# Down projections of a hybrid decoder trunk: the weights' differences and low parts moved from GpSimd to VectorE

## The chip, the cores and the metric

The kernel runs on one core of a Trainium2 chip. The metric is device time in microseconds (us). A core has five engines with an in-order queue each: TensorE (PE in the profile; PEld is its weight load), VectorE (DVE), ScalarE (ACT), GpSimd (POOL) and SyncE (SP), which here issues nearly all DMAs. The engines run side by side and wait for one another through semaphores.

## The reference

Two layers over 16 meta tokens and 1024 tokens of width 1024, all in float32: a Mamba-2 mixer and a convolutional gated FFN, then stick-breaking attention and a second FFN. What the change touches is the last product of each FFN, the down projection:

```
D_MODEL, D_FF, FFN_CONV = 1024, 2816, 3

def _conv_ffn(u, w_up, conv_w, conv_b, w_down):
    h = _causal_dwconv(u @ w_up, conv_w, conv_b)
    g, val = jnp.split(h, 2, axis=-1)
    return (jax.nn.silu(g) * val) @ w_down

for layer in range(DEPTH):          # DEPTH = 2
    ...                             # layer 0: SSD mixer; layer 1: attention
    h = h + _conv_ffn(_rmsnorm(h, ffn_norm[layer]), ffn_w_up[layer], ...,
                      ffn_w_down[layer])
```

## The kernel before, in words

**Three products for one.** TensorE multiplies a rounded float32 format (F32R). To keep float32 precision, each operand is split into a rounded high part and the rest: ScalarE copies `x` into `hi` with the rounding, and another engine makes `lo = x - hi`. `mm3` (from L153) then issues three matmuls: high by high (L156), weights' high by the tokens' low part (L157), weights' low by the tokens' high part (L158).

**Stages.** The kernel runs the mixer, the up projection of layer 0 (`up`), its down projection (`down`), the attention, and `up` and `down` of layer 1. Token tiles have F = 260 columns in layer 0 and 256 in layer 1.

**The down projection.** `down` (from L946) takes the first 16 of the 22 blocks of 128 of the inner width and multiplies them with a Strassen-Winograd scheme: the tokens' half-matrices are `b11, b12, b21, b22` (two token halves by two halves of the inner width), the weights' are `a11` to `a22`, and seven products (i = 1, 7, 6, 5, 3, 4, 2, in this order) take the place of eight. There are two rounds, and in each round two sets (`Set`, x = 0 and 1) whose products are summed in PSUM: 28 operand sets per down, 14 pairs. The rows that remain (`rows`, six blocks) are multiplied in the ordinary way at the end (`weights`, `tokens`), while `sums` adds the seven sums into the stream.

`operands(i)` makes what one product of one set needs. In place, on tiles of 128 x 1024, it forms the difference of weights (L989, L992, L995, L998; on GpSimd as `pt`) and of tokens (L990, L993, L996, L1000; on VectorE as `tt`). Then come four instructions: ScalarE rounds the weights (L1004, `wh`), GpSimd makes their low part (L1005, `wl`), ScalarE rounds the tokens (L1006, `gh`), VectorE makes their low part (L1007, `gl`). `wh` and `wl` have three buffers each. In `weights` (L1062, L1063) the ordinary blocks are split in the same way, the low part on GpSimd.

`part` issues the matmuls of one accumulator: per operand set 48 matmuls of 260 columns in layer 0 (eight accumulators, all eight PSUM banks), 24 of 512 columns in layer 1 (four). After the second set of a pair, `add` (L1052, L1054) empties the bank: VectorE adds it to a sum in SBUF, or, where a sum begins (products 1, 5, 6 and 7 in the first round), ScalarE copies it. The sums of `sums` are L1024, the rounding and low parts of `tokens` are L1073 and L1074. GpSimd also makes the differences and low parts of the up projection's weights (`up_weights`, L859 and nearby), and VectorE its convolutions and sums (L282, L901, L909).

**Order.** Outside the attention, the order on each engine is set by a planner that lays the instructions out by its own costs when the kernel is built. One edge is set by hand: `behind_up` ties an instruction behind `last_up`, the last product of the up projection's gate on VectorE (L901), without a semaphore, so that in the same engine's queue it comes after it. Before the change it holds the tokens' first difference of product 7 (L990).

Of the kernel before, what the change touches and what calls it, by code (L numbers as in the profile page):

```python
# [8 lines left out]
F32 = mybir.dt.float32  # L9
# [60 lines left out]
class Trunk:  # L70
# [875 lines left out]
    def down(self, layer, gd, hd, pool, after):  # L946
# [3 lines left out]
        nc, a, F = self.nc, self.a, FNS[layer]  # L950
        H, S = D // 2, 2 * F
        parts = [(0, S)] if S <= 512 else [(0, F), (F, F)]
        tt = nc.vector.tensor_tensor
        pt = nc.gpsimd.tensor_tensor
        ADD, SUB = ALU.add, ALU.subtract
        half = lambda j: slice(S - S * j, 2 * S - S * j)

        def behind_up(ins):

            nosync = mybir.DependencyInfo(mybir.DependencyClass.NoSync, mybir.DependencyReason.DATA)  # L960
            self.tc.add_manual_dep(ins.ins, self.last_up.ins.name, nosync, reason="behind the up projection")

        def pair(t, w):
            return t[:, : 2 * w].rearrange("p (q c) -> p q c", q=2)

        class Set:
# [16 lines left out]
            def operands(me, i):  # L983

                b, w = me.b, me.w
                b11, b12, b21, b22 = b[0, 0], b[0, 1], b[1, 0], b[1, 1]
                a11, a12, a21, a22 = w[0, 0], w[0, 1], w[1, 0], w[1, 1]
                if i == 7:
                    pt(a21, a11, a21, op=SUB)  # L989
                    behind_up(tt(b12, b22, b12, op=SUB))  # L990
                elif i == 6:
                    pt(a21, a22, a21, op=SUB)  # L992
                    tt(b11, b11, b12, op=ADD)  # L993
                elif i == 5:
                    pt(a11, a11, a21, op=ADD)  # L995
                    tt(b12, b22, b11, op=SUB)  # L996
                elif i == 3:
                    pt(a21, a12, a21, op=SUB)  # L998
                elif i == 4:
                    tt(b11, b21, b11, op=SUB)  # L1000
                x, y = {1: (b11, a11), 7: (b12, a21), 6: (b11, a21), 5: (b12, a11), 3: (b22, a21), 4: (b11, a22), 2: (b21, a12)}[i]
                gh, gl = (pair(self.Q(z, F32R), QW // 2)[:, :, :S] for z in ("gh", "gl"))
                wh, wl = (self.wp.tile([P, 1024], F32R, tag=z, name=self.nm(z)) for z in ("wh", "wl"))
                nc.scalar.activation(wh, y, AF.Copy)  # L1004
                pt(wl, y, wh.bitcast(F32), op=SUB)  # L1005
                nc.scalar.activation(gh, x, AF.Copy)  # L1006
                tt(gl, x, gh.bitcast(F32), op=SUB)  # L1007
                return gh, gl, wh, wl
# [50 lines left out]
        def weights(b, hi, lo):  # L1059
            w32 = self.wp.tile([P, 1024], F32, tag="w32", name=self.nm("w32"))  # L1060
            nc.sync.dma_start(w32, a["w_down"][layer, b])
            nc.scalar.activation(hi, w32, AF.Copy)  # L1062
            pt(lo, w32, hi.bitcast(F32), op=SUB)  # L1063
            ws.append((hi, lo))

        def tokens(x):
# [23 lines left out]
        for m in range(0, len(plan), 2):  # L1090
            r, i, _ = plan[m]
            last = r + 1 == len(rounds)
            ps = {}
            if r == 0 and i == 7:
                for f in range(KD):
                    nc.sync.dma_start(h[f][:, : 2 * S] if f < 4 else h[f][:, half(0)], hd[f] if f < 4 else hd[f, :, half(0)])
            if last and i == 2:
                h22 = [self.Q("h22") for _ in range(2)]
                h22 = [h22[f // 2][:, f % 2 * S : f % 2 * S + S] for f in range(4)]
                for f in range(4):  # L1100
                    nc.sync.dma_start(h22[f], hd[4 + f, :, half(1)])
            for x in range(2):
                make(m + x + 1)
                if last and i == 4 and x:
                    weights(rows[0], *own())
                if last and i == 2 and not x:
                    tokens(0)
                    weights(rows[1], *own())
                    weights(rows[2], *(self.Q(z, F32R)[:, :D] for z in ("wh", "wl")))
                    for b in rows[3:]:  # L1110
                        weights(b, *common())
                for t, f in ((t, f) for t in range(len(parts)) for f in range(4)):
                    if x == 0:
                        ps[t, f] = next(kinds)("acc")
                    part(ps[t, f], made[m + x], f, t, x == 0)
                    if x == 1:
                        add(i, f, t, ps.pop((t, f)), r == 0)
                del made[m + x]
# [445 lines left out]
```

## Time and profile before

| | |
|---|---|
| median of 3 runs | 3022.47 us (3021.38 to 3026.99) |
| the profiled execution | 3024.83 us, of which the span of the trace is 3023.1 us |
| granted TensorE clock, mean | 0.981 |
| first down projection in the trace | first matmul at 1356.7 us |
| second down projection in the trace | first matmul at 2752.82 us |

How to read the profile: times count from the start of the span. A row of the timeline gives start and duration in us, engine, line, operation, output and inputs with their shapes, and the number of instructions merged; in brackets the idle time of the engine before it and what ended that. A row of the windows gives from and to, length, busy time of an engine with its count of instructions, the clock that TensorE was granted (1.00 is full), the share of time that the DMA engines were busy, and GB/s. A row of waits names who waited for whom: total us, times, longest. A row of groups gives line, engine, operation, count, then total busy us and mean ns of one, then idle time before. TensorE's matmuls are pipelined: one lasts longer than the distance between two starts.

### The profile page before, as it was taken

The numbers are of one execution on the slowest core, as the hardware profiler recorded it, in microseconds if no ns is written. First come the engines' busy times: TensorE is split into PE (matmuls) and PEld (weight loads), VectorE is DVE, ScalarE is ACT, GpSimd is POOL, SyncE is SP. The second block draws the span as 40 slices with busy tenths as digits, with TensorE's granted clock in tenths as the row PEclk, the third lists the DMA queues.
The fourth block names the chain that finished last, engine by engine and source line by source line (L and its number), as shares of the span: only waits on it lengthen the run. The fifth ranks groups of instructions, "written<-read, shape, count | busy, mean of one in ns | idle before, by whom it ended". The sixth has DMA issues, their size and how long they took to land.

```text
span 3023.1 us, 57199 instructions
## 1 busy us (share of the span) xinstructions
PE 2875.1 (95%) x21855; PEld 2733.1 (90%) x21855; DVE 2158.8 (71%) x3994; ACT 1621.9 (54%) x3308; POOL 1403.3 (46%) x1282
## 2 busy tenths in 40 slices
PE   7999999989989999998999999999997999998988
PEld 4998998889979999998998999999797999997778
DVE  5686868875376665568966888888748665568895
ACT  4555555553245555554334888877735555554432
POOL 1254444532415666658733222222234676667751
PEclk9999999999999999999999999999998999999999
DMA  5243323313222222243132222221331222225231
GB/s 161 75 118 86 109 78 111 113 53 139 74 78 64 78 80 77 84 160 132 47 117 72 60 65 65 68 59 52 129 112 64 85 76 79 77 84 176 91 105 56
DMA packets 125891, 272.76 MB, mean 90 GB/s; under 512 B 15888, under 2 KB 55440, under 8 KB 125616
## 3 DMA queue, kind: packets, MB, share of 16 engines
q1 hardware_dynamic: 120304, 258.17, 27.1%
q10 hardware_dynamic: 4048, 6.36, 0.6%
q0 software_dynamic: 1264, 4.57, 0.4%
q8 instruction: 172, 2.82, 0.4%
q14 instruction: 103, 0.84, 0.1%
HBM read 200.93 MB, written 53.21 MB: 84 GB/s over the span
## 4 chain that ended last, share of the span: by engine, by line
PE 52%; DVE 13%; ACT 4%; issue 3%; DMA 2%; POOL 0%; SPq 0%; DVEq 0%; ACTq 0%; POOLq 0%
PE p L156 9%; PE p L157 9%; PE p L158 9%; PE acc L157 4%; PE acc L156 4%; PE acc L158 4%; DVE gl L1007 3%; PE po L1314 2%; PE pj L156 2%; PE pj L158 2%; PE pj L157 2%; PE lg L1272 1%; DVE kp L1285 1%; PE wT L1299 1%; ACT kp L1275 1%
## 5 line engine op out<-in xcount | busy, mean ns | idle before, releaser
L156 PE MATMUL pj<-uh,wh 128*128 128x348 f32 (+2 forms) x1536 | 507.3, 331 | 16.1 <-DVE qs L1223 7.1
L157 PE MATMUL pj<-ul,wh 128*128 128x348 f32 (+2 forms) x1536 | 498.7, 325 | 0.0
L158 PE MATMUL pj<-uh,wl 128*128 128x348 f32 (+2 forms) x1536 | 496.2, 323 | 0.0
L157 PE MATMUL p<-bl,fh 128*128 128x262 f32 (+1 forms) x1408 | 401.0, 285 | 14.0 <-DVE bl L827 14.0
L156 PE MATMUL p<-bh,fh 128*128 128x262 f32 (+1 forms) x1408 | 401.3, 286 | 4.2 <-ACT fh L858 3.5
L158 PE MATMUL p<-bh,fl 128*128 128x262 f32 (+1 forms) x1408 | 399.3, 284 | 0.0
L859 POOL TENSOR_TENSOR fl<-x,fh 128x1024 fp32r<-128x1024 f32 x88 | 212.7, 2418 | 306.4 <-ACT fh L858 277.5
L150 POOL TENSOR_TENSOR wl<-w,wh 128x1024 fp32r<-128x1024 f32 (+2 forms) x80 | 164.6, 2060 | 327.1 <-ACT wh L149 327.0
L156 PEld LDWEIGHTS pj<-uh,wh 128*128 128x128 f32 x1536 | 292.0, 190 | 23.8 <-DVE qs L1223 9.2
L157 PE MATMUL p<-bl,wh 128*128 128x262 f32 (+1 forms) x1056 | 301.8, 286 | 8.5 <-DVE bl L827 8.5
L156 PE MATMUL p<-bh,wh 128*128 128x262 f32 (+1 forms) x1056 | 301.9, 286 | 6.3 <-ACT bh L826 6.3
L158 PE MATMUL p<-bh,wl 128*128 128x262 f32 (+1 forms) x1056 | 301.2, 285 | 0.0
L157 PEld LDWEIGHTS pj<-ul,wh 128*128 128x128 f32 x1536 | 292.6, 190 | 1.4 <-issue 0.5
L158 PEld LDWEIGHTS pj<-uh,wl 128*128 128x128 f32 x1536 | 291.9, 190 | 0.3 <-issue 0.2
L157 PEld LDWEIGHTS p<-bl,fh 128*128 128x128 f32 x1408 | 268.0, 190 | 16.1 <-DVE bl L827 15.9
L282 DVE SCALAR_TENSOR_TENSOR c<-p,params,c 128x260 f32<-128x260 f32 (+1 forms) x440 | 207.9, 481 | 94.4 <-ACT c L278 92.6
L156 PEld LDWEIGHTS p<-bh,fh 128*128 128x128 f32 x1408 | 268.4, 191 | 6.0 <-ACT fh L858 3.9
L158 PEld LDWEIGHTS p<-bh,fl 128*128 128x128 f32 x1408 | 267.4, 190 | 0.1
L157 PE MATMUL acc<-gl,wh 128*128 128x260 f32 (+1 forms) x672 | 217.9, 326 | 19.8 <-DVE gl L1007 19.8
L909 DVE TENSOR_TENSOR p<-p,ft 128x262 f32<-128x262 f32 (+1 forms) x176 | 76.8, 436 | 221.6 <-ACT ft L906 128.9
L384 DVE TENSOR_TENSOR h<-h,acc 128x256 f32<-128x256 f32 (+4 forms) x232 | 102.6, 450 | 175.1 <-PE acc L158 172.5
L156 PE MATMUL acc<-gh,wh 128*128 128x260 f32 (+1 forms) x672 | 215.0, 325 | 8.7 <-DVE p L1054 5.4
(309 smaller groups left out, 8539.4 us busy)
## 6 DMA issues: line engine op xcount, KB each, us to landing
w<-in_w_up SPq DMA_DIRECT2D x88, 512.0 KB
w<-in_w_down SPq DMA_DIRECT2D x44, 512.0 KB
w<-in_w_in SPq DMA_DIRECT2D x40, 512.0 KB
E<-ea_d SPq DMA_DIRECT2D x32, 464.0 KB
D<-acs_d SPq DMA_DIRECT2D x32, 420.5 KB
g<-c SPq DMA_DIRECT2D x88, 130.0 KB
g<-c SPq DMA_DIRECT2D x88, 128.0 KB
b<-g SPq DMA_DIRECT2D x16, 520.0 KB
```

The lines of the kernel that those rows point to most:

```text
L150: nc.gpsimd.tensor_tensor(wl[:, :n], w32[:, :n], wh[:, :n].bitcast(F32), op=ALU.subtract)
L156: mm(out, wh, uh, start=first, stop=False, skip_group_check=joins)
L157: mm(out, wh, ul, start=False, stop=False, skip_group_check=joins)
L158: mm(out, wl, uh, start=False, stop=last, skip_group_check=joins)
L282: nc.vector.scalar_tensor_tensor(to, ps[:, o + i : o + i + n], wcol(i), out, op0=ALU.mult, op1=ALU.add)
L384: self.nc.vector.tensor_tensor(h[f][:, o], h[f][:, o], ps[:, :n], op=ALU.add)
L859: tt(lo[:, :n], t, hi[:, :n].bitcast(F32), op=ALU.subtract)
L909: add = lambda o, x, y: tt(o[:, :N], x[:, :N], y[:, :N], op=ALU.add)
L1007: tt(gl, x, gh.bitcast(F32), op=SUB)
L1272: nc.tensor.matmul(ps[:nt, :m], part[:, c0 : c0 + nt], ks[a][:, s0 : s0 + m], start=x == 0, stop=x == 1)
L1275: nc.scalar.activation(kp[:nt, :m], ps[:nt, :m], AF.Sigmoid, scale=self.rt[2][:nt, i : i + 1])
L1314: nc.tensor.matmul(po[64 * a : 64 * a + 64, w], v[: CH[c][1], c, 64 * a : 64 * a + 64], wt[a][: CH[c][1], c, :nt], start=x == 0, stop=x == ...
```

## The change

In `down`, the name `pt` (GpSimd) goes, and everything that it did is done by VectorE (`tt`): the four kinds of weight differences, the low parts `wl` of every operand set, and the low parts of the ordinary blocks. GpSimd has no instruction left in `down`. The first weight difference of product 7 is tied behind the up projection's last VectorE instruction, as the tokens' difference next to it was already.

```
-        pt = nc.gpsimd.tensor_tensor
...
                 if i == 7:
-                    pt(a21, a11, a21, op=SUB)
+                    behind_up(tt(a21, a11, a21, op=SUB))
                     behind_up(tt(b12, b22, b12, op=SUB))
                 elif i == 6:
-                    pt(a21, a22, a21, op=SUB)
+                    tt(a21, a22, a21, op=SUB)
                     tt(b11, b11, b12, op=ADD)
                 elif i == 5:
-                    pt(a11, a11, a21, op=ADD)
+                    tt(a11, a11, a21, op=ADD)
                     tt(b12, b22, b11, op=SUB)
                 elif i == 3:
-                    pt(a21, a12, a21, op=SUB)
+                    tt(a21, a12, a21, op=SUB)
...
                 nc.scalar.activation(wh, y, AF.Copy)
-                pt(wl, y, wh.bitcast(F32), op=SUB)
+                tt(wl, y, wh.bitcast(F32), op=SUB)
                 nc.scalar.activation(gh, x, AF.Copy)
                 tt(gl, x, gh.bitcast(F32), op=SUB)
...
             nc.scalar.activation(hi, w32, AF.Copy)
-            pt(lo, w32, hi.bitcast(F32), op=SUB)
+            tt(lo, w32, hi.bitcast(F32), op=SUB)
             ws.append((hi, lo))
```

More of the change, by code (lines that the diff above doesn't have):

```diff
@@ L953, in down @@
         tt = nc.vector.tensor_tensor
-        pt = nc.gpsimd.tensor_tensor
         ADD, SUB = ALU.add, ALU.subtract
@@ L988, in operands @@
                 if i == 7:
-                    pt(a21, a11, a21, op=SUB)
+                    behind_up(tt(a21, a11, a21, op=SUB))
                     behind_up(tt(b12, b22, b12, op=SUB))
                 elif i == 6:
-                    pt(a21, a22, a21, op=SUB)
+                    tt(a21, a22, a21, op=SUB)
                     tt(b11, b11, b12, op=ADD)
                 elif i == 5:
-                    pt(a11, a11, a21, op=ADD)
+                    tt(a11, a11, a21, op=ADD)
                     tt(b12, b22, b11, op=SUB)
                 elif i == 3:
-                    pt(a21, a12, a21, op=SUB)
+                    tt(a21, a12, a21, op=SUB)
                 elif i == 4:
@@ L1004, in operands @@
                 nc.scalar.activation(wh, y, AF.Copy)
-                pt(wl, y, wh.bitcast(F32), op=SUB)
+                tt(wl, y, wh.bitcast(F32), op=SUB)
                 nc.scalar.activation(gh, x, AF.Copy)
@@ L1062, in weights @@
             nc.scalar.activation(hi, w32, AF.Copy)
-            pt(lo, w32, hi.bitcast(F32), op=SUB)
+            tt(lo, w32, hi.bitcast(F32), op=SUB)
             ws.append((hi, lo))
```

## The prediction

> **What bounds the kernel now.** I read the page first: span, busy shares.
>
> ```profile
> span 3023.1 us, 57199 instructions
> PE 2875.1 (95%) x21855; PEld 2733.1 (90%) x21855; DVE 2158.8 (71%) x3994; ACT 1621.9 (54%) x3308; POOL 1403.3 (46%) x1282
> ```
>
> The profiled execution took 3024.83 us; the sum below starts there. The median shown, 3022.47, lies 2.4 us lower, inside the spread of the three runs. TensorE is the bound nearly everywhere, so a change is worth what it takes from TensorE's waits. So next come the stretches of the two down projections, TensorE alone: length, busy time (matmuls), granted clock, then DMA.
>
> ```profile
> 1365.00:1405.00 40.00, 30.03 (x228) 0.91 0.17 68
> 1425.00:1430.00 5.00, 4.43 (x35) 1.00 0.44 159
> 1430.00:1460.00 30.00, 30.00 (x254) 1.00 0.29 89
> 1460.00:1505.00 45.00, 39.61 (x312) 0.96 0.04 13
> 1530.00:1550.00 20.00, 16.79 (x125) 0.91 0.52 168
> 2765.00:2800.00 35.00, 25.19 (x98) 0.90 0.17 57
> 2805.00:2870.00 65.00, 65.00 (x282) 1.00 0.31 104
> 2870.00:2875.00 5.00, 3.14 (x14) 1.00 0.00 2
> 2900.00:2910.00 10.00, 9.32 (x37) 1.00 0.32 108
> 2925.00:2945.00 20.00, 14.59 (x90) 0.83 0.37 130
> ```
>
> 1430 to 1460 and 2805 to 2870 are undisturbed: 254/30 = 8.47 matmuls per us (260 columns) and 282/65 = 4.34 (512 columns). At those rates the matmuls of the other stretches would need less time than they took. The losses, idle and lower clock together:
> First down: 40 - 228/8.47 = 13.1 (start), 0.9 and 45 - 312/8.47 = 8.2 (middle), 20 - 125/8.47 = 5.2 (tail): 27.4 us.
> Second down: 35 - 98/4.34 = 12.4 (start), 1.8 and 1.5 (middle). The tail mixes widths, so I take idle 5.4 plus 14.59 x 0.17 = 2.5 for the clock: 7.9. Together 23.6 us.
> So 51.0 us is all that better operands could return. Who is waited for, the first three rows in the first down, the others in the second (total, times, longest):
>
> ```profile
> PE acc L157 <- DVE gl L1007: 10.0, 4, 5.6
> PE acc L156 <- DVE p L1054: 5.4, 4, 2.7
> PE acc L156 <- DVE h L1054: 3.7, 4, 1.8
> ...
> PE acc L157 <- DVE gl L1007: 9.8, 4, 4.9
> PE acc L158 <- POOL wl L1005: 2.4, 2, 1.9
> ```
>
> VectorE (gl, and the adds of L1054 that empty the banks) is late, GpSimd seldom. That looks like a reason not to give VectorE more. The timeline of the two engines says otherwise (start, duration).
>
> ```profile
> 1346.22 1.24 DVE L1007 TENSOR_TENSOR gl<-b,gh 128x1040 fp32r<-128x1040 f32 x1 [3.35 <-ACT gh L1006]
> 1347.38 0.43 DVE L909 TENSOR_TENSOR p<-p,ft 128x262 f32<-128x262 f32 x1
> 1361.20 6.16 DVE L990 TENSOR_TENSOR b<-b,b 128x1040 f32<-128x1040 f32 x2
> 1370.61 3.39 DVE L1007 TENSOR_TENSOR gl<-b,gh 128x1040 fp32r<-128x1040 f32 x1
> 1373.92 3.40 DVE L993 TENSOR_TENSOR b<-b,b 128x1040 f32<-128x1040 f32 x1
> 2757.16 6.14 DVE L990 TENSOR_TENSOR b<-b,b 128x1024 f32<-128x1024 f32 x2
> ...
> 1337.56 2.40 POOL L1005 TENSOR_TENSOR wl<-w,wh 128x1024 fp32r<-128x1024 f32 x1 [0.30 <-ACT wh L1004]
> 1369.55 3.35 POOL L1005 TENSOR_TENSOR wl<-w,wh 128x1024 fp32r<-128x1024 f32 x1
> 1372.86 3.37 POOL L995 TENSOR_TENSOR w<-w,w 128x1024 f32<-128x1024 f32 x1
> ```
>
> The same gl takes 1.24 us with GpSimd idle (the next instruction starts 1.16 later) and 3.39 while GpSimd runs beside it. GpSimd's own goes from 2.40 to 3.35. One instruction on each engine thus takes 3.31 us start to start; two on VectorE alone would take 2.32. Moving work *to* the late engine should make it earlier.
>
> **The change, part by part.**
>
> *Moved: low parts.*
>
> ```profile
> L1005 POOL TENSOR_TENSOR wl<-w,wh 128x1024 fp32r<-128x1024 f32 x56 | 162.1, 2902 | 99.6 <-ACT wh L1004 99.6
> ```
>
> 56 here, and by the code 12 of L1063 and 32 differences (L989, L992, L995, L998; 16 per down): 100 instructions. VectorE gains 100 x 1.16 = 116 us and loses the stretching, about 2.2 us on each gl or b that overlapped. All of it must hide under the matmuls, so it is judged by rate. TensorE's rate from its timeline:
>
> ```profile
> 1356.70 0.28 PE L156 MATMUL acc<-gh,wh 128*128 128x260 f32 x1
> 1357.41 0.28 PE L156 MATMUL acc<-gh,wh 128*128 128x260 f32 x1
> 1374.05 0.59 PE L157 MATMUL acc<-gl,wh 128*128 128x260 f32 x1 [5.62 <-DVE gl L1007]
> ...
> 2762.80 0.39 PE L157 MATMUL acc<-gl,wh 128*128 128x512 f32 x1
> 2763.73 0.39 PE L158 MATMUL acc<-gh,wl 128*128 128x512 f32 x1
> 2769.99 0.79 PE L157 MATMUL acc<-gl,wh 128*128 128x512 f32 x1 [4.95 <-DVE gl L1007]
> ```
>
> Six starts in 0.71 us are 0.118 each; an operand set has 48 matmuls, 5.7 us. In the second down four starts in 0.93 make 0.2325; 24 matmuls, 5.6 us.
>
> *Start.* Up's last VectorE work ends at 1361.2; the tie puts the difference of a21 behind it, where GpSimd did it during the up stage. Product 1 of both sets keeps TensorE busy from 1356.70 for 2 x 5.7 = 11.4 us, to 1368.1. Now gl starts at 1370.61 and TensorE goes on at 1374.05. After: a21 and b12 of both sets, 4 x 1.16 from 1361.2, end at 1365.8, and wl and gl of the first set at 1368.2. ScalarE's two roundings lie under the second set's differences. So even in the poorer order the stall is near 0.1 us; with one or two differences of product 6 ahead of gl (as L993 could be) 1 to 2.5. The second down has the same order: free at 2757.2, six instructions later 2764.2, and TensorE's work lasts to 2769.99 - 4.95 = 2765.0. I keep 1.5 us of each start. After that products 7, 6 and 5 need 4 x 1.16 = 4.6 us of VectorE per set (ScalarE empties the banks in this round) against 5.7: VectorE gets ahead. Returned: 11.6 + 10.9 = 22.5.
>
> *Middle (second round).* VectorE also empties banks:
>
> ```profile
> 1459.87 2.75 DVE L1007 TENSOR_TENSOR gl<-b,gh 128x1040 fp32r<-128x1040 f32 x1
> 1462.55 0.75 DVE L1054 TENSOR_TENSOR p<-p,acc 128x260 f32<-128x260 f32 x2
> 1473.29 2.77 DVE L1007 TENSOR_TENSOR gl<-b,gh 128x1040 fp32r<-128x1040 f32 x1
> ```
>
> From one pair's gl to the next pair's is 13.4 us now. After: 8 x 1.16 + 8 adds of at most 0.375 = 12.3, against 11.4 of TensorE: still short by 0.9 in each of three pairs, 2.7 us, part of it covered because operands are made up to two sets ahead (wh and wl have three buffers). In products 3, 4, 2 and 1, with one difference per set or none, VectorE needs at most 10. The second down's four adds of twice the width I put at the same 3.0, against 2 x 5.6. I keep 2.0 and 1.5 of the 9.1 and 3.3: returned 8.9.
>
> *Tail.* The last low parts (L1063) ran beside the sums of L1024:
>
> ```profile
> 1530.67 2.22 DVE L1024 TENSOR_TENSOR h<-h,p 128x520 f32<-128x520 f32 x1
> 1535.92 1.30 DVE L1024 TENSOR_TENSOR h<-h,p 128x520 f32<-128x520 f32 x2
> ...
> 1529.40 5.71 POOL L1063 TENSOR_TENSOR wl<-w,wh 128x1024 fp32r<-128x1024 f32 x2 [0.83 <-ACT wh L1062]
> ```
>
> Two of L1063 stretched the L1024 beside them from 0.65 to 2.22; on VectorE they cost 2 x 1.16 themselves. Bounds: nothing returned, or all 13.1 of both tails. Nearest row: two stretched sums (3.1) against 2.3 of new work, a small gain, but the waits on POOL wl go too. I take half: 6.5.
>
> *Up's end.* The wl of product 1 is not tied. Two per down now lie between up's convolutions on VectorE, which idles 3.35 us ahead of the gl at 1346.22, so cost 0 to 2 x 1.16 per down. I take 1.2 each: -2.4. No DMA is moved, and SP's queue is passed by nothing. w and b tiles come free earlier, so the second round's loads may start earlier; the start has the room for them (DMA share 0.17 in both).
>
> Sum: 22.5 + 8.9 + 6.5 - 2.4 = 35.5 us, 3024.8 - 35.5 = 2989 us. Of 51.0, 13.1 stays.
>
> *The clock.* After the 5.62 us wait a matmul lasts 0.59, and the stretch shows 0.91; but 1460 to 1505 shows 0.96 although its longest wait is 2.7, and lost 8.2 with 5.4 idle. So I let short waits cost clock too: about a third of the 13.1 that stays. The Trainium skill, "TensorE: Matmul & The Clock Gate" (Part 1, the HAM clock gate), has the clock halve only after an idle window of about 3.4 us; the first row agrees, the second speaks for more than that. By the rule the waits I leave, all shorter, would cost no clock, and the time would be some 4 us lower, 2985, an estimate from that page.
>
> **Rivals.**
> (a) *VectorE becomes the bound.* For: 12.3 against 11.4, one in-order queue for operands, adds and sums. Then middle and tails stay as they are, a start keeps 3 us: returned 25.5 - 6 - 2.4 = 17, 3008 us. Against: the queue is slower today.
> (b) *No change.* The first low parts go early into VectorE's queue and hold up's convolutions:
>
> ```profile
> 1356.99 1.06 ACT L1004 ACTIVATE wh<-w 128x1024 fp32r<-128x1024 f32 x1 [0.73 <-DMA w<-in_w_down]
> ```
>
> wl of set 2 needs this wh (end 1358.05). Put ahead of the convolutions of 1349, it would hold them 9 to 10 us per down, and the starts return little: 35.5 - 2 x 10 - 13 = 3, 3022 us. Against: ScalarE's order stands 0.73 us off the landing, so the planner knows the load's time.
> (c) *Slower: adds behind waiting operands.* wl waits for wh, wh for TensorE to free a buffer; GpSimd bore 99.6 us of that. If VectorE's queue has wl and gl ahead of the adds that free the next product's banks, TensorE waits 2 x 1.16 + 1.06 = 3.4 us per pair. There are 28 pairs; it decides from 35.5/28 = 1.3 us per pair on. If every second pair pays, 47.6 - 35.5 = 12: 3037 us. Against: gl has the same wait already, right behind.
>
> **How the numbers follow.** Mine 0.65, (a) 0.17, (b) 0.08, (c) 0.10. 0.2% (6 us) is about what a measurement tells from no change. Faster 0.82, same 0.08, slower 0.10. The low end is all 51 returned less a little, 2976; the high end reaches past (a), to 3014, which leaves (b) and (c) out. Mine alone: 2976 to 3001.
>
> **What would show it.** gl, b, w and wl on VectorE near 1.2 us in both downs; no GpSimd there. The matmul after product 1 follows with under 2.5 us of wait, and the 40 us from there hold about 320 matmuls, not 228, at full clock. Middle: waits on L1054 of 1 to 3 us. I am wrong if VectorE's instructions stay above 2 us (the stretching had another cause), if L1054 is waited for in every pair, or if up's end slides later than 1361 and 2757.

## The result, and the profile after

| | before | after |
|---|---|---|
| median | 3022.18 us (4 runs, 3021.38 to 3026.99) | 2971.34 us (4 runs, 2970.31 to 2975.13) |
| ratio, with its 95% interval | | 0.9829 (0.9817 to 0.9840) |
| the profiled execution | 3024.83 us, span 3023.1 us | 2970.31 us, span 2968.4 us |
| granted TensorE clock, mean | 0.981 | 0.988 |

The change returns 50.8 us by the medians, 1.7%. The kernel is faster, as forecast, but by 17.7 us more than forecast, and its time lies 4.7 us below the low end of the range. In the changed kernel the lines of `down` stand one lower (`wl` is L1004, `gl` L1006, `add` L1051 and L1053, the differences L988 to L999, the tail's low part L1062).

First the page of the kernel after: span, and busy time of each engine.

```profile
span 2968.4 us, 57155 instructions
PE 2853.7 (96%) x21855; PEld 2718.1 (92%) x21855; DVE 2121.7 (71%) x4094; ACT 1622.3 (55%) x3308; POOL 1110.3 (37%) x1182
```

VectorE has 100 instructions more and is busy 37 us less. The 100 take 100 x 1.22 = 122 us there, so everything else on VectorE became 159 us shorter: 1.6 us for each instruction that left GpSimd.

Next the windows of the kernel after, TensorE alone, over the stretches that the prediction summed (from and to, length, busy with its count of matmuls, clock, DMA share, GB/s).

```profile
1365.00:1405.00 40.00, 38.92 (x323) 1.00 0.45 155
1430.00:1460.00 30.00, 30.00 (x253) 1.00 0.00 1
1460.00:1505.00 45.00, 45.00 (x378) 1.00 0.33 107
1505.00:1550.00 45.00, 45.00 (x377) 1.00 0.36 118
2730.00:2745.00 15.00, 14.38 (x61) 1.00 0.57 209
2765.00:2800.00 35.00, 35.00 (x152) 1.00 0.49 164
2805.00:2870.00 65.00, 65.00 (x281) 1.00 0.22 73
2870.00:2910.00 40.00, 40.00 (x296) 1.00 0.25 80
```

The 40 us from 1365 hold 323 matmuls where they held 228. By the same rates the starts now lose 40 - 323/8.47 = 1.9 us and 15 - 61/4.34 = 0.9 us. Middle and tail of the first down lose 45 - 378/8.47 = 0.4 and 45 - 377/8.47 = 0.5, which is the error of the reading (253 matmuls in the undisturbed 1430 to 1460 make 8.43, not 8.47). The second down loses nothing behind its start (152/35 = 4.34, and 281/65 = 4.32 where its second round begins), and the clock is full in every row. So 3.7 us of the 51.0 are left. The lengths agree. From its first matmul to the attention's first score matmul, the first down took 284.5 us and takes 258.3. From its first matmul to the first transpose of the output, the second took 216.7 and takes 191.3. Together that is 51.6 us less. (Some 4 us of these lie outside the stretches that I summed. The two profiled executions differ by 54.5; one lies 2.6 us above its median, the other 1.0 below.)

The waits of the kernel after, for TensorE alone, from 1340 to 1420 and from 2700 to 2790, one row each (total, times, longest):

```profile
PE acc L157 <- DVE gl L1006: 1.1, 1, 1.1
...
PE acc L157 <- DVE gl L1006: 0.5, 1, 0.5
```

These two are all the waits on operands and banks that are left in both downs; 5.6 and 4.9 us stood in their places. The timeline of VectorE at the first start shows the order that the prediction worked out:

```profile
1357.21 1.23 DVE L1004 TENSOR_TENSOR wl<-w,wh 128x1024 fp32r<-128x1024 f32 x1 [2.37 <-ACT wh L1003]
1360.42 1.22 DVE L988 TENSOR_TENSOR w<-w,w 128x1024 f32<-128x1024 f32 x1
1361.55 1.24 DVE L989 TENSOR_TENSOR b<-b,b 128x1040 f32<-128x1040 f32 x1
1364.99 1.22 DVE L1004 TENSOR_TENSOR wl<-w,wh 128x1024 fp32r<-128x1024 f32 x1
1366.13 1.23 DVE L992 TENSOR_TENSOR b<-b,b 128x1040 f32<-128x1040 f32 x1
1367.28 1.24 DVE L1006 TENSOR_TENSOR gl<-b,gh 128x1040 fp32r<-128x1040 f32 x1
```

Every instruction takes 1.22 to 1.24 us and the next starts 1.13 to 1.15 later. One difference of product 6 (L992) stands ahead of `gl`, the case for which the prediction had 1 to 2.5 us of stall. TensorE's timeline there shows how the order shortens it: the first matmuls of product 7 in all eight accumulators, which need no `gl`, stand ahead of the first that needs it. Before the change only one stood there.

```profile
1366.03 1.46 PE L156 MATMUL acc<-gh,wh 128*128 128x260 f32 x8
1368.57 0.39 PE L157 MATMUL acc<-gl,wh 128*128 128x260 f32 x1 [1.08 <-DVE gl L1006]
```

The groups of `gl` in the first down, before and after (busy, mean ns):

```profile
L1007 DVE TENSOR_TENSOR gl<-b,gh 128x1040 fp32r<-128x1040 f32 x28 | 63.4, 2269 | 17.3 <-ACT gh L1006 13.5 <-PE acc L157 3.4
```
```profile
L1006 DVE TENSOR_TENSOR gl<-b,gh 128x1040 fp32r<-128x1040 f32 x28 | 34.6, 1240 | 2.2 <-ACT gh L1005 2.0 <-PE acc L157 0.2
```

In the second round of the first down, TensorE had waited for VectorE's adds. Now VectorE enters that round behind a wait for TensorE (1431.75, the last adds of the first round), works without an idle time until 1467, and waits for TensorE again at 1468.47 (timeline of VectorE, kernel after):

```profile
1424.47 1.43 DVE L1053 TENSOR_TENSOR h<-h,acc 128x260 f32<-128x260 f32 x4
...
1431.75 0.43 DVE L1053 TENSOR_TENSOR h<-h,acc 128x260 f32<-128x260 f32 x1 [1.80 <-PE acc L158]
...
1468.47 0.42 DVE L1053 TENSOR_TENSOR p<-p,acc 128x260 f32<-128x260 f32 x1 [1.20 <-PE acc L158]
```

### The profile page after: what moved, and what is told of

Its sections match the earlier page's. It is cut to its first block, busy times and chain, and to the rows that moved or that the text cites. A ratio compares the mean times of both kernels' runs of the same rounds, so it can differ in the third digit from the quotient of the medians.

```text
span 2968.4 us, 57155 instructions
## 1 busy us (share of the span) xinstructions
PE 2853.7 (96%) x21855; PEld 2718.1 (92%) x21855; DVE 2121.7 (71%) x4094; ACT 1622.3 (55%) x3308; POOL 1110.3 (37%) x1182
## 4 chain that ended last, share of the span: by engine, by line
PE 77%; DVE 11%; ACT 5%; issue 3%; POOL 2%; DMA 2%; SPq 0%; DVEq 0%; ACTq 0%; POOLq 0%
PE p L156 10%; PE p L157 10%; PE p L158 10%; PE acc L157 7%; PE acc L158 7%; PE acc L156 7%; PE pj L156 5%; PE pj L157 5%; PE pj L158 5%; PE po L1313 2%; PE lg L1271 2%; PE wT L1298 1%; DVE kp L1284 1%; ACT kp L1274 1%; ACT bt L1275 1%
## 5 line engine op out<-in xcount | busy, mean ns | idle before, releaser
L157 PE MATMUL acc<-gl,wh 128*128 128x260 f32 (+1 forms) x672 | 211.4, 320 | 1.7 <-DVE gl L1006 1.6
L157 PEld LDWEIGHTS p<-bl,wh 128*128 128x128 f32 x1056 | 201.4, 191 | 10.1 <-DVE bl L827 10.0
```

The source lines that it names most:

```text
L157: mm(out, wh, ul, start=False, stop=False, skip_group_check=joins)
```

## The experiments

Two theories stood against each other. **Blocking:** an instruction of VectorE is held while GpSimd reads SBUF (the on-chip memory that both work on) beside it, so the cure is that GpSimd is silent. **Latency:** `wl` comes sooner because VectorE makes it in 1.22 us instead of 2.40 or more, and the stretching is a by-product. Each ratio is to the kernel before, in brackets its interval. Differences in us are between medians unless they are said to be by the ratios; the two can differ by a few us.

**1. The low parts alone** (kernel before; the 32 differences stay on GpSimd).

```
-                pt(wl, y, wh.bitcast(F32), op=SUB)
+                tt(wl, y, wh.bitcast(F32), op=SUB)
...
-            pt(lo, w32, hi.bitcast(F32), op=SUB)
+            tt(lo, w32, hi.bitcast(F32), op=SUB)
```

> Only the 68 low parts go to VectorE; the 32 weight differences stay on GpSimd. Blocking theory (an instruction with two SBUF inputs on VectorE and one on GpSimd hold each other up; the changed kernel is fast because nothing is left to collide): 77 us of GpSimd work remain instead of 240, all in products 7, 6, 5 and 3. There a set needs 3 x 1.16 on VectorE and 2.4 on GpSimd, one after the other 5.9 against TensorE's 5.7: nearly enough. Tails return whole (13 us), starts and middles mostly: about 2985, 37 of the 51 us. Rival (GpSimd is only slow: 2.4 us of latency on the chain of each operand): the differences are one to two steps ahead, the low part is last on the chain, so nearly all 51 return: 2971 to 2975.

Measured: 2988.70 us, 0.9876 (0.9861 to 0.9891). All low parts are on VectorE, and still 0.0047 of 3022 = 14 us are missing. Groups and TensorE's waits of this run:

```profile
L1007 DVE TENSOR_TENSOR gl<-b,gh 128x1040 fp32r<-128x1040 f32 x28 | 45.4, 1623 | 2.9 <-ACT gh L1006 2.5 <-PE acc L157 0.4
```
```profile
PE acc L157 <- DVE gl L1007: 8.3, 4, 3.1
PE acc L156 <- DVE p L1054: 4.3, 3, 2.2
```

`gl` stays stretched, and what TensorE waits for is VectorE. GpSimd's latency on the low parts cannot explain this, for GpSimd makes none here; the 32 differences that it still makes can.

**2. The differences alone** (the changed kernel with both low parts back on GpSimd).

```
-                tt(wl, y, wh.bitcast(F32), op=SUB)
+                pt(wl, y, wh.bitcast(F32), op=SUB)
...
-            tt(lo, w32, hi.bitcast(F32), op=SUB)
+            pt(lo, w32, hi.bitcast(F32), op=SUB)
```

> Only the 32 differences go to VectorE (with the tie); the 68 low parts stay on GpSimd. Blocking theory: 163 us of GpSimd work remain, in every set and in the tails; products 7, 6 and 5 need 3 x 1.16 + 2.4 = 5.9 per set, and the adds read PSUM and are not held up; the tails return nothing (13 stay): about 2993, 29 of the 51 us. Rival (latency only): the 2.4 us on the chain stay in every set, gains under 15 us: 3007 or more.

Measured: 3018.19 us, 0.9975 (0.9964 to 0.9987). The number is nearer to the latency theory. Timeline of the two engines at the first start of this run, and its waits:

```profile
1361.68 1.23 DVE L990 TENSOR_TENSOR b<-b,b 128x1040 f32<-128x1040 f32 x1
...
1363.97 3.44 DVE L990 TENSOR_TENSOR b<-b,b 128x1040 f32<-128x1040 f32 x1
...
1362.98 6.70 POOL L1005 TENSOR_TENSOR wl<-w,wh 128x1024 fp32r<-128x1024 f32 x2 [2.30 <-ACT wh L1004]
```
```profile
PE acc L156 <- DVE h L1054: 11.3, 7, 3.9
PE acc L157 <- DVE gl L1007: 11.2, 5, 4.2
```

The same instruction takes 1.23 us ahead of GpSimd's `wl` and 3.44 beside it. TensorE waits for VectorE's adds and `gl`, hardly for GpSimd's low parts (2.5 us in all; 4.4 us in the kernel before). My sum for this run had left out the adds of the second round: with a low part on GpSimd a set needs 5.9 us there, and its share of the adds 1.3 more, against 5.7 of TensorE. That is where the sum fell short; the waits are those of blocking.

**3. Blocking by itself.** The changed kernel, with all of the downs' work on VectorE, plus useless GpSimd work for every operand set: a one-column copy that places it in time, and additions in an idle tile that read SBUF.

```
+                nc.gpsimd.tensor_copy(idle[:, :1], wh[:, :1].bitcast(F32))
+                for _ in range(6):
+                    nc.gpsimd.tensor_tensor(idle[:, 2:], idle[:, 2:], idle[:, 2:], op=ADD)
```

> The changed kernel, and for each operand set GpSimd gets six additions of 128 x 262 from SBUF to SBUF on a scratch tile that nobody needs (about 4.5 us of GpSimd per set of 5.7 us; what it had before was 2.4 to 4.8 per set), started after the set's wh by a copy of one column. Blocking theory: gl, wl and the differences on VectorE stretch from 1.2 to 2 us and more, and most of the gain goes: 3005 to 3050. Latency rival: nobody waits for this work, so the time stays at 2971 to 2976. Order rival (the planner's new order made the gain): 2971 to 2980 as long as the order stays.

Measured: 3053.04 us, 1.0091 (1.0076 to 1.0106): 82 us more than the changed kernel, with the same useful work. It is not clean. An addition took 1.09 us on average, so six took 6.5 us per set, where TensorE needs 5.7. GpSimd fell behind, and ScalarE's `wh` waited for it (the release of the buffer that the copy reads), 207 us in all. So two more runs.

**4. GpSimd busy without reads**: 12 memsets in place of the 6 additions (`nc.gpsimd.memset(idle[:, 2:], 0.0)`).

> The same with twelve memsets of 128 x 262 on the scratch tile in place of the six additions: GpSimd about as busy, but it reads nothing from SBUF. Blocking by reads: VectorE's instructions stay at 1.2 us, 2971 to 2976. If any GpSimd access holds VectorE up: as the run with the additions, 3005 or more. Latency rival: 2971 to 2976.

Measured: 2974.22 us, 0.9837 (0.9820 to 0.9853), no loss that can be told. Groups of this run, then both engines in its first down:

```profile
L1007 POOL MEMSET idle<- 128x262 f32 x672 | 213.0, 317 | 35.8
L1003 ACT ACTIVATE wh<-w 128x1024 fp32r<-128x1024 f32 x56 | 59.4, 1062 | 150.3 <-POOL idle L1005 74.6 <-POOL idle L1007 64.7 <-DVE w L991 4.2
L1009 DVE TENSOR_TENSOR gl<-b,gh 128x1040 fp32r<-128x1040 f32 x28 | 34.5, 1237 | 1.9 <-ACT gh L1008 1.8
```
```profile
1369.86 5.55 POOL L1007 MEMSET idle<- 128x262 f32 x15
...
1372.49 2.39 DVE L1009 TENSOR_TENSOR gl<-b,gh 128x1040 fp32r<-128x1040 f32 x2
...
1375.36 14.41 POOL L1005 COPY idle<-wh 128x1 f32<-128x1 f32 x1
```

GpSimd is busy 213 us with writes, and `gl` takes 1.237 us as if it were idle; the two at 1372.49 stand right beside memsets. Here too `wh` waits for the copy and the memsets, 139 us, and that costs nothing. The copy, which reads one column, shows the other side of the blocking: this one took 14.41 us, until VectorE, which had worked without a gap beside it at 1.22 to 1.25 us each, paused at 1389.7.

**5. Half as many reads**: 3 additions in place of 6.

> The run with idle additions, with three per operand set in place of six. In that run the wait of wh for GpSimd's one-column copy (207 us in all) mixed in: GpSimd had fallen behind. Three additions are at most 3.3 us of 5.7, so GpSimd keeps up and only the collisions are left. Blocking theory: gl, wl and the differences stretch from 1.22 to 1.4 us and more, VectorE's 4.6 us per set in products 7, 6 and 5 becomes 5.5 to 7: 2985 to 3010. If the slowdown came from GpSimd's backlog alone: 2971 to 2977.

Measured: 2998.90 us, 0.9915 (0.9901 to 0.9929), 28 us lost. Groups, the same place in the first down, and waits:

```profile
L1007 POOL TENSOR_TENSOR idle<-idle 128x262 f32<-128x262 f32 x168 | 185.4, 1104 | 11.1
L1009 DVE TENSOR_TENSOR gl<-b,gh 128x1040 fp32r<-128x1040 f32 x28 | 39.3, 1406 | 2.2 <-ACT gh L1008 1.9 <-PE acc L157 0.2
```
```profile
1374.79 15.77 POOL L1007 TENSOR_TENSOR idle<-idle 128x262 f32<-128x262 f32 x10
...
1377.43 3.24 DVE L1009 TENSOR_TENSOR gl<-b,gh 128x1040 fp32r<-128x1040 f32 x2
```
```profile
PE acc L157 <- DVE gl L1009: 11.9, 10, 2.7
PE acc L156 <- DVE h L1059: 4.7, 5, 1.6
```

GpSimd is busy for less time than with the memsets (185 against 213 us), and `wh` waits for GpSimd less (86 against 139 us). Yet two `gl` beside additions take 3.24 us instead of 2.39, `gl` and the adds are late, and TensorE waits. Reads do it, time on GpSimd does not. The Trainium skill, "SBUF — State Buffer" (Who interferes with whom), says this: VectorE's second pair of ports is the only one of GpSimd and is locked by one of them at a time, so that an instruction of VectorE with two inputs in SBUF contends with one of GpSimd that reads. Runs 4 and 5 agree (`gl` 1.237 us on average with the writes, 1.406 with the 168 reading additions).

**6. The tail alone** (kernel before, only the 12 low parts of `weights` on VectorE).

```
-            pt(lo, w32, hi.bitcast(F32), op=SUB)
+            tt(lo, w32, hi.bitcast(F32), op=SUB)
```

> The kernel before, with only the 12 low parts of the ordinary blocks (L1063) made by VectorE: the tails alone. The prediction's term was half of the tails' loss, 6.5 us, which gives about 3016 (against a median near 3022 to 3026: ratio 0.998). If the whole loss of the tails (13.1 us) came from these 12 colliding with the sums of L1024, about 3010 (ratio 0.9957). If the tails gain only because the rounds before them come out earlier, no change.

Measured: 3016.63 us, 0.9975 (0.9966 to 0.9984), 7.6 us less by the ratio. Its trace agrees: the lengths of the two downs, taken as above, are 279.2 and 213.3 us, 8.6 less than before.

**7. The tail alone undone** (the reverse edit, in the changed kernel):

> The changed kernel with the 12 low parts of the ordinary blocks (L1062) back on GpSimd: the counterpart of the run with the tail alone, which returned about 7.6 us. If the tails' loss is their own, it comes back in the same size: 2978 to 2979. If VectorE now reaches the tails without a backlog and has room for the collisions, less: 2971 to 2975. If the whole 13 us hang on these 12: 2984.

Measured: 2978.34 us, 0.9849 (0.9835 to 0.9864), 7.0 us more than the changed kernel (6.0 by the ratios). Its trace puts only about half of that in the downs: 260.5 and 192.8 us, 3.7 more than in the changed kernel, with 3.2 us of waits in the tails. The rest lies ahead of the downs and between them, where the edit changes nothing. So the tail's own instructions are worth 3.7 to 8.6 us, around the 6.5 that I took. But the changed kernel's tails lose at most 0.5 us, where 13.1 were lost. By this sum some 4 to 9 us of the tails' losses belong to the rounds before and return when those are on time; no run shows that part alone.

**8. Without the tie** (the changed kernel).

```
-                    behind_up(tt(a21, a11, a21, op=SUB))
+                    tt(a21, a11, a21, op=SUB)
```

> The changed kernel without the tie on the first weight difference (the tokens' difference keeps its own). VectorE idles 3.4 us near the end of the up stage and two differences take 2.3, so if the planner puts them there, the 1.1 us wait before product 7 goes and nothing else moves: 2970, within 2 us of the changed kernel. If the tie is needed, the differences push the convolutions, up's last block ends 1 to 2.5 us later in each stage, and TensorE waits for it: 2973 to 2977.

Measured: 2972.84 us, 0.9829 (0.9816 to 0.9843). The tie makes no difference that these runs can tell.

**9. One set ahead instead of two**: the changed kernel with one buffer of `wh` and one of `wl` held through the rounds, so that the sets have two of each.

```
+        held = [self.wp.tile([P, 1024], F32R, tag=z, name=self.nm(z)) for z in ("wh", "wl")]
+        for x in held:
+            behind_up(nc.vector.tensor_copy(x[:, :4], self.zero))
...
+                for x in held:
+                    nc.vector.tensor_copy(x[:, 4:8], x[:, :4].bitcast(F32))
```

> The changed kernel with one of the three wh and one of the three wl buffers held from the start of each down projection to the last product, so that operands can be made one set ahead instead of two. The prediction let 2.0 and 1.5 us of the middle stay, because VectorE needs 12.3 us per pair of products 7, 6 and 5 and TensorE 11.4; the changed kernel shows no wait there. If running two sets ahead covers it, waits of 1 to 3 us per pair come back: 2976 to 2990. If VectorE's need is simply smaller than I put it, the time stays: 2970 to 2974.

Measured: 2985.91 us, 0.9876 (0.9859 to 0.9892), 15 us lost. The number is the one that I expected if two sets ahead cover the middle. The place of the loss is another. TensorE's waits on operands in this run's first down, then its second, and the window of the second round in its first down:

```profile
PE acc L158 <- DVE wl L1004: 4.5, 1, 4.5
...
PE acc L156 <- ACT wh L1003: 1.6, 1, 1.6
...
PE acc L156 <- ACT wh L1003: 6.1, 2, 4.5
```
```profile
1460.00:1505.00 45.00, 45.00 (x378) 1.00 0.23 74
```

All these waits lie at the starts of the downs (the last ones end at 1364.3 and 2739.8), and the middle holds 378 matmuls in 45 us, as with three buffers. The third buffer matters at the starts (12.2 us of waits here, 1.6 in the changed kernel); the middle does without it. That theory of mine fell.

**10 and 11. The same cure one stage earlier.** TensorE's largest wait on operands that is left stands at the start of each up projection, where GpSimd splits weights beside VectorE's normalisation and convolution. Waits, and both engines there, of the changed kernel:

```profile
PE p L157 <- DVE bl L827: 22.5, 6, 6.7
```
```profile
877.86 0.43 DVE L837 TENSOR_TENSOR ft<-h,ft 128x262 f32<-128x262 f32 x1
...
880.92 2.15 DVE L763 TENSOR_SCALAR y<-y 128x260 f32<-128x260 f32 x1
882.99 2.63 DVE L837 TENSOR_TENSOR ft<-h,ft 128x262 f32<-128x262 f32 x1
...
880.18 5.14 POOL L859 TENSOR_TENSOR fl<-x,fh 128x1024 fp32r<-128x1024 f32 x2 [28.13 <-ACT fh L858]
```

So `up_weights` of the first block, then of the first two, goes to VectorE as well (the second run has `if b > 1`).

```
-        tt = nc.gpsimd.tensor_tensor
+        tt = nc.gpsimd.tensor_tensor if b else nc.vector.tensor_tensor
```

> The changed kernel, and the weights of the first block of each up projection (seven instructions of up_weights in line 844 and behind) made by VectorE too. In the changed kernel TensorE waits 22.5 us for bl (L827) at the start of the up stages; there VectorE is busy without a gap, and from 880.9 to 896.5 its 12 short instructions take 15.5 us beside GpSimd's, where they take 0.34 to 0.43 each alone, some 4 to 5. Blocking theory: on VectorE the eight cost 6.4 us themselves, so bl is ready about 4 to 5 us earlier in each stage: 2961 to 2963. Rival (VectorE is the bound there and GpSimd is not in its way): 6.4 us more per stage, 2984.

Measured: 2968.29 us, 0.9805 (0.9789 to 0.9821): 3.0 us less than the changed kernel by the medians, 7 by the ratios, where I had expected 8 to 10. The `bl` waits fell from 22.5 to 9.0 us, but those on `bh` rose from 7.1 to 18.5. In the first up projection GpSimd's five instructions for the second block start where they started (886.5, and 886.7 in the changed kernel). VectorE reaches the second half's factors earlier (L761 at 891.3 instead of 896.4) and now meets them there: that L761 takes 2.27 us instead of 0.42, and the five end at 898.8 instead of 894.9. That this is what delays `bh` is argued, not shown.

> The run with the first block's weights of the up projections on VectorE, with the second block's too. In that run five GpSimd instructions of the second block had moved up to where VectorE makes the second half's factors: L761, L763, L764 and one L827 took 6.0 us there instead of 1.6. Blocking theory: 4 us less per stage until the products of the second half, minus what the eight instructions (6.4 us) cost where VectorE is the bound: between 2960 and 2968. If VectorE's own time decides: 2972 to 2980.

Measured: 2959.80 us, 0.9792 (0.9778 to 0.9807), 11.5 us below the changed kernel: the fastest of all. Its waits:

```profile
PE p L157 <- DVE bl L827: 12.4, 8, 4.3
PE p L156 <- ACT bh L826: 9.8, 4, 4.7
```

Of the 29.6 us on `bl` and `bh` in the changed kernel, 22.2 are still there.

## Why the prediction was too small

**Right:** the cause (runs 3 to 5), its sign, the reading of 51.0 us as all that better operands could return, and the starts. Kept there: 3.0 us; measured: 1.9 + 0.9. `gl`, `b`, `w` and `wl` are all near 1.2 us, and no rival decided: VectorE is not the bound, it waits for TensorE on both sides of the second round's heavy products. That 51.0 and 50.8 lie so close is partly luck: 3.7 us of the 51.0 stayed, and some 4 came from outside the stretches that I summed.

**The step that failed is "Of 51.0, 13.1 stays".** The mechanism was right; the losses that I let stay, and the charge at up's end, were put too high. 3.7 us stayed. By the terms:

- *Middle, kept 2.0 + 1.5, measured 0.4 and 0.* I needed 12.3 us of VectorE per pair from 1.16 and at most 0.375; measured are 1.14 and (4 adds in 1.43) 0.33 start to start, 8 x 1.14 + 8 x 0.33 = 11.8 against 11.4. That would be 1.2 us behind after three pairs. But the sum also counted product 7's four differences in the second round, and the trace has them in the first (L988 at 1392.44 and 1402.85, L989 at 1411.18 and 1418.46), where VectorE had idle time: 4.6 us less. The waits on the adds of 1 to 3 us that I expected are not there. That the second set of lead isn't needed is shown (run 9); that the work done ahead covers the rest is argued.
- *Tails, kept 6.6, measured at most 0.5.* This is the largest term. "I take half" was a choice between two bounds, and it is luck that it lies inside what the tail's own instructions are worth (3.7 to 8.6 us, runs 6 and 7). The failure was to treat the tail as if the rounds ahead stayed late.
- *Up's end, charged 2.4 beside the 3.0 of the starts; together they measured 2.8.* The delay is real on VectorE: the `wl` at 1357.21 stands ahead of up's last work and waits 2.37 us for `wh`, which is rival (b) on a small scale. Up's last instruction there ends 5.9 us behind the down's first matmul (1360.4 and 1354.5) instead of 4.5 (1361.2 and 1356.7). But TensorE has 11.4 us of product 1 by then, and what is left uncovered is the same wait for `gl` that the starts had been charged with. I counted one wait twice.
- *The clock.* I let a third of what stays be clock. With one wait of 1.1 us left, the stretch shows 1.00, so there was nothing to lose. The runs speak for short waits costing clock, as I had it: in run 1 a wait of 2.1 us (1366.2 to 1368.3, on `gl`) is followed by a clock of 0.50 from 1369.4 to 1372.8. The rule of the Trainium skill that I set beside it ("TensorE: Matmul & The Clock Gate", Part 1), which asks for an idle window of about 3.4 us, would leave the clock full there. The measurement decides, and it is luck that the rule's 2985 came nearer.

Together 3.1 + 6.1 + (5.4 - 2.8) = 11.8 us of the 17.7. Another 2.6 us is that the sum starts from a profiled execution that much above its median. The 3.3 that are left are near the 4 us outside the stretches that I summed. The range had the same fault: its low end, "all 51 returned less a little", lay above the plain result of its own reading, 3024.8 - 51.0 = 2973.8.

**Every instruction left on GpSimd costs.** By ratios, the loss against the changed kernel is 51.7 us with 100 instructions on GpSimd, 44 with 88 (run 6), 44 with 68 (run 2), 14 with 32 (run 1) and 6 with 12 (run 7): 0.4 to 0.65 us for each, however the work is divided.

## What to carry to other kernels

When the engine that is late shows one instruction at two durations, look at what the other engine does at those moments before taking work away from the late one: here giving VectorE 100 instructions more made it earlier, since GpSimd's reads beside it had cost more than the work. Move such work whole, for what is left behind goes on costing (runs 1, 2 and 7) and can meet other work of the late engine (run 10). And when a mechanism explains all of the waits, let the forecast's range reach to all of the loss; residues kept for safety need a row of their own.

## What the runs showed of the hardware

- A two-input instruction of VectorE that meets a reading one of GpSimd became longer by about GpSimd's whole instruction: 1.23 became 3.44 us beside a `wl` that takes 2.40 alone (run 2). The trace shows all of it as busy.
- The holding goes both ways: GpSimd's `wl` goes from 2.40 to 3.35 us in the kernel before, and a one-column copy took 14.41 us beside a VectorE that did not pause (run 4).
- The one-input scalar instruction is held too: L763 on 260 columns took 2.15 us at 880.92 beside GpSimd, 0.30 the second time (897.4), in the kernel after.
- VectorE's adds with one input in PSUM (`add`, 260 columns) are not held: 0.417 us on average in run 2, 0.424 in the kernel after.
- GpSimd's memsets hold nothing that these traces show: 672 of them, and `gl` at 1.237 us (run 4).
- TensorE's clock was halved behind a single wait of 2.1 us (run 1, 0.50 from 1369.4 to 1372.8).
